# Causal attention with two full-height logit products, and the causal mask added beforehand to the subtracted row

## The chip, the cores and the metric

The kernel runs on one core of a Trainium2 chip. The metric is the device time of one execution in microseconds. A core has TensorE (PE, the products; PEld are its weight loads), VectorE (DVE), ScalarE (ACT), GpSimd (POOL) and SyncE (SP), which here issues the DMAs. Each engine works through its own queue in order and waits on semaphores for the others.

## The reference

One layer of a streaming encoder: 1024 tokens, 1024 channels, float32. A normalised input is projected once, and the columns are shared among four mixers of 256 channels each: A (mLSTM), B (causal pooling), C (RWKV) and D (forgetting attention); each has a gate, and the four go through one output projection. A cross-attention into 256 memory tokens follows. The change concerns D:

```python
def forgetting_attention(q, k, v, f_pre, qk_g):
    q = rms_norm(q, qk_g[0]) * (dh ** -0.5)
    k = rms_norm(k, qk_g[1])
    log_f_cum = jnp.cumsum(jax.nn.log_sigmoid(f_pre), axis=-1)
    for blk in range(s_len // 128):
        q0, q1 = blk * 128, (blk + 1) * 128
        logits = einsum("bhtd,bhsd->bhts", q[:, :, q0:q1], k[:, :, :q1])
        logits = logits + log_f_cum[:, :, q0:q1, None] - log_f_cum[:, :, None, :q1]
        causal = (q0 + arange(128))[:, None] >= arange(q1)[None, :]
        p = softmax(where(causal, logits, -inf))
        outs.append(einsum("bhts,bhsd->bhtd", p, v[:, :, :q1]))
```

with 4 heads of 64 channels. The term with the query's own F is the same for all keys of a row and falls out of the softmax, so the kernel subtracts only the row F of the keys.

## The kernel before, in words

**Stages.** The memory side and the first normalisation come first, then the projections of C and its recurrence. From about 480 to 565 us follow A, B and the operands of D; from 565 to 735 us attention D, into which the output projection is woven; then the cross-attention. Products in float32 precision are made of three passes with numbers split into a high and a low part: `mm3` (lines L137, L138, L139) takes high x high, high x low, low x high.

**Operands of D.** `foxop(n)` makes them, per head h. A query tile `qst[h]` of 128 rows holds the 64 channels of a head twice, as high part in one half and low part in the other; `kh[h]` holds the high part of the keys in both halves. So one product of full height (128 rows) gives q_high x k_high + q_low x k_high. The low part of the keys, `kl`, is kept once: two heads share a tile, each in one half (L1136 subtracts 64 rows). `Fb[h]` is the row F of a head, broadcast to all partitions by DMA (L1170); two heads lie side by side in one tile.

**A logit step.** `flog(g)` handles one query tile i (128 queries) and one head h, g = 4i + h. For each chunk of up to 512 of the (i+1) x 128 keys it writes one bank: L1226, the product of full height; L1227, 64 rows high, q_high x k_low; and, in the last chunk, L1229, a product of the identity with a mask that adds -1e30 above the diagonal of the last 128 columns. DVE then subtracts `Fb` and keeps the maximum (L1230), negates it (L1233), and ACT takes the exponential (L1234). `ftr(g)` transposes the weights (L1244) into a `pt` tile, `fav(g)` multiplies two heads by the values (L1257), `fin(i)` divides by the sums (L1264 to L1267) and `tgate(i)` gates the other mixers' outputs (L1206 to L1211).

**Order.** PE's instructions in D stand in an order written by hand: `flog` of the next step, two fillers, `ftr`, on even steps `fav`, then fillers again. Fillers are triples of L137 to L139: first the gate projection of D (`zgemm`, evacuated by L754 to L759), then the output projection of the tile before. DVE, ACT, POOL and SP take their instructions in the order of a scheduler with priorities. `wout(q)` loads the output weights (L1281) into `wr` and `zu` buffers and splits them (L1283 on ACT, L1284 on DVE or POOL). L126 on POOL or L124 on DVE make the low parts of the earlier weights.

**Ahead of D** on POOL stand, for each of the last chunks of A, a reciprocal root (L143, L144), for which DVE's L1067 waits, and the product with the norm's weights (L1068). DVE's evacuations of the pooling (L1119) and of `zgemm` (L754) stand behind L1067 in its queue.

Of the kernel before, what the change touches and what calls it, by code (L numbers as in the profile page):

```python
# [9 lines left out]
F32R = mybir.dt.float32r  # L10
AF = mybir.ActivationFunctionType
ALU = mybir.AluOpType
# [6 lines left out]
D = 1024  # L19
# [17 lines left out]
def tile_trunk(ctx: ExitStack, tc: tile.TileContext, a, out, dbg=None):  # L37
# [48 lines left out]
    def f32(ap):  # L86
        return ap.bitcast(F32)
# [9 lines left out]

    # ---------------------------------------------------------------- helpers
    wcount = {"wr": 0, "wh": 0, "wl": 0}
# [83 lines left out]

    # ---------------------------------------------------------------- first loads
    pr0 = tc.cur_priority
# [17 lines left out]

    # ---------------------------------------------------------------- memory side and pre norm
    mss = m0.one("mss", [128, 2])
# [73 lines left out]

    # ---------------------------------------------------------------- constants  # L280
    incl = m0.one("incl", [128, 128])
# [37 lines left out]

    # ---------------------------------------------------------------- VW = V wo per head  # L320
    def vwprep(h):
# [64 lines left out]
    def defer(n, f):  # L386
        """run f when n more of the pending projections' products are emitted."""
        after.append([n, f])

    def fill(n):  # L390
        """emit n of the pending projections' products here."""
        while n > 0 and fillers:
            try:
                w = next(fillers[0]) or 1
            except StopIteration:
                fillers.pop(0)
                continue
            n -= w
            for d in after:
                d[0] -= w  # L400
            for d in [d for d in after if d[0] <= 0]:
                after.remove(d)
                d[1]()

    def tgemm(c0, nt, evac):
        """nt tiles of 128 channels, all tokens, channels on partitions."""
        p = [[ps("mm", [128, 512]) for _ in range(2)] for _ in range(nt)]
        kk = 4 // nt
        w = wpiece(w_in, c0, nt * 128, kk)
        for _ in range(8 // kk):  # L410
            ws = [next(w) for _ in range(kk)]
            for c in range(nt):
                cs = slice(c * 128, (c + 1) * 128)
                for k, wh, wl in ws:
                    for hf in range(2):
                        mm3(p[c][hf], wh[:, cs], wl[:, cs], *hslice(k, hf * 512, 512), k == 0, k == 7)
                        yield
        for c in range(nt):
            with tc.high_priority():
                evac(c, p[c])  # L420
# [9 lines left out]
    def ngemm_q(wd, c0, n, act, evac):  # L430
        """all tokens x n columns, a bank to a token tile."""
        w = []
        for i0, ni in ((0, 2), (2, 2), (4, 4)):
            p = [ps("mm", [128, 512]) for _ in range(ni)]
            for k, wh, wl in (wpiece(wd, c0, n, 2) if i0 == 0 else w):
                if i0 == 0:
                    w.append((k, wh, wl))
                for i in range(ni):
                    mm3(p[i][:, 0:n], *act(i0 + i, k), wh, wl, k == 0, k == 7)
                    yield 0.5  # L440
            for i in range(ni):
                with tc.high_priority():
                    evac(i0 + i, p[i][:, 0:n])

    def ngemm_h(wd, c0, act, evac, nt=4):
        """all tokens x 256 columns, nt token tiles at a time."""
        w = []
        for t0 in range(0, NT, nt):
            p = [ps("mm", [128, 2, 256]) for _ in range(nt // 2)]
            for k, wh, wl in (w or wpiece(wd, c0, 256, 2)):  # L450
                if t0 == 0 and nt < NT:
                    w = w + [(k, wh, wl)]
                for i in range(nt):
                    mm3(p[i // 2][:, i % 2, :], *act(t0 + i, k), wh, wl, k == 0 and i % 2 == 0, k == 7, True)
                    yield
            for i in range(nt):
                evac(t0 + i, p[i // 2][:, i % 2, :])
# [3 lines left out]

    # ---------------------------------------------------------------- C projections
    shifted, act = [None] * 7, {}
# [28 lines left out]
    def cnorm(hf, j):  # L492
        """the keys of a head divided by their length."""
        ck, hs = shifted[2 + j], slice(hf * 512, (hf + 1) * 512)
# [232 lines left out]

    # ---------------------------------------------------------------- other projections
    def vgemm(c0, n, gc0, dst):
# [97 lines left out]

    # ---------------------------------------------------------------- gate rows, (token tile, head) on partitions
    fd = dp.tile([32, 128], F32, name="fd")
# [174 lines left out]

    # ---------------------------------------------------------------- mixers A and B, operands of D
    da = Pool("da", {"q": 4, "k": 4, "kl": 2})
    am = Pool("am", {"v": 2, "e": 3, "nu": 2, "hh": 2, "hsq": 1, "ks": 2})
# [9 lines left out]

    ab = Pool("ab", {"u": 8})
    # ---------------------------------------------------------------- A
    aqT, akT = [[t[:, q, :] for q in range(2)] for t in aqk]  # L1020
# [62 lines left out]

    # ---------------------------------------------------------------- B
    ub = []
# [35 lines left out]

    qst, kh, kl = [None] * 4, [None] * 4, [None] * 2

    def foxop(n):
        """queries (n < 4) as a stack of both parts, keys as two copies of the first part and the second part."""
        h = n % 4
        r1, r2 = PH[h % 2], PH[1 - h % 2]
        raw = ab("u", [128, 1024])
        for r in PH:
            SY.dma_start(raw[r], rT[(n // 4) * 256 + h * 64:(n // 4) * 256 + (h + 1) * 64, :])  # L1130
        hi = da("k" if n >= 4 else "q", [128, 1024], F32R)
        SC.copy(hi, raw)
        if n >= 4:
            if h % 2 == 0:
                kl[h // 2] = da("kl", [128, 1024], F32R)
            V.tensor_tensor(kl[h // 2][r1], raw[r1], f32(hi[r1]), op=ALU.subtract)  # L1136
            kh[h] = hi
        else:
            V.tensor_tensor(hi[r2], raw[r2], f32(hi[r2]), op=ALU.subtract)
            qst[h] = hi  # L1140
# [4 lines left out]
    with tc.manual_schedule(engines={PE}):  # L1145
# [17 lines left out]
        while fillers:  # L1163
            fill(1)
    Fb = []
    for h in range(4):
        if h % 2 == 0:
            fb2 = eh("t", [128, 2, 1024])
        t = fb2[:, h % 2, :]
        SY.dma_start(t.rearrange("p (a b) -> p a b", a=8),  # L1170
                     bass.AP(tensor=fd.tensor, offset=fd.offset + h * 128, ap=[[0, 128], [512, 8], [1, 128]]))
        Fb.append(t)
    ab.close()
    am.close()
    db = Pool("db", {"v": 2, "lg": 2, "pt": 4, "rE": 1})
    identr, maskN = db.one("identr", [128, 128], F32R), db.one("maskN", [128, 128], F32R)
    V.tensor_copy(identr, ident)
    V.tensor_scalar(maskN, maskD, NEG, None, op0=ALU.mult)
    dv = [db("v", [128, 4, 256]) for _ in range(2)]
    for q in range(2):  # L1180
        SY.dma_start(dv[q], dvd.rearrange("(q i p) c -> q p i c", q=2, p=128)[q])

    # ---------------------------------------------------------------- D and the output projection
    p0 = Pool("p0", {"ld": 1, "zt": 1, "act": 2})
# [29 lines left out]
    def flog(g):  # L1214
        i, h = divmod(g, 4)
        j, x = divmod(h, 2)
        ts, n, r1 = slice(i * 128, (i + 1) * 128), (i + 1) * 128, PH[x]
        if h == 0:
# [4 lines left out]
        for k, c0 in enumerate(range(0, n, 512)):  # L1223
            c1 = min(c0 + 512, n)
            p = ps("lg", [128, 512])
            T.matmul(p[:, 0:c1 - c0], qst[h][:, ts], kh[h][:, c0:c1], start=True, stop=False)  # L1226
            T.matmul(p[:, 0:c1 - c0], qst[h][r1, ts], kl[j][r1, c0:c1], start=False, stop=c1 < n)  # L1227
            if c1 == n:
                T.matmul(p[:, i * 128 - c0:n - c0], identr, maskN, start=False, stop=True)  # L1229
            V.tensor_tensor_reduce(lg[:, c0:c1], p[:, 0:c1 - c0], Fb[h][:, c0:c1], 1.0, prev, ALU.subtract, ALU.max, mx[:, k:k + 1])  # L1230
            prev = mx[:, k:k + 1]
        ng = base("tf", [128, 1])
        V.tensor_scalar(ng, prev, -1.0, None, op0=ALU.mult)  # L1233
# [81 lines left out]
    with tc.manual_schedule(engines={PE}):  # L1315
# [72 lines left out]

        # ------------------------------------------------------------ memory attention
        gcols = [cst[:, 184 + k:185 + k] for k in range(8)]  # L1390
# [6 lines left out]
        def qgemm(g):  # L1397
            """the queries of a head, channels on partitions."""
            w = []
# [123 lines left out]
def _pack(a):  # L1523
    """An identity and the vectors that go along partitions, 128 channels to a column; the pool weights as diagonal blocks."""
    import numpy as np
# [32 lines left out]
```

## Time and profile before

Three runs of the kernel took 984.74, 983.16 and 980.48 us, the median being 983.16. The profile was taken in one more execution.

| | |
|---|---|
| span of the profiled execution | 981.5 us |
| median of the runs | 983.16 us |
| PE busy | 929.1 us, 95% of the span, 6089 products |
| DVE busy | 578.9 us, 59% |
| ACT busy | 419.6 us, 43% |
| POOL busy | 252.9 us, 26% |
| A, B and operands of D, 480 to 565 us | PE busy 79.61 of 85.00 |
| D and output projection, 600 to 690 us | PE busy 90.00 of 90.00 |
| mask products L1229 in D | 32, 328 ns each by the profile |
| half-height products L1227 in D | 48, 324 to 496 ns each by width |

In a row of the timeline stand the start, the duration, engine, line and operation, what is written and read, the shape, and in brackets the idle time before it with what ended it. Products overlap in PE's pipeline and their ends are modelled, so the time that a product takes is read from one start to the next, not from its duration. Rows by line give the busy time of the group and the mean of one in ns; rows of waits give the sum, the number and the longest.

### The profile page before, as it was taken

Reading aid. Unit: us, or ns where it says so; the run is one execution under the profiler, and the core shown is the slowest. Engines: PE = TensorE matmul, PEld = TensorE weight load, DVE = VectorE, ACT = ScalarE, POOL = GpSimd, SP = SyncE. Lnnn points to the kernel's source line nnn. Section 1 sums busy time; section 2 is a strip of 40 time slices with the busy share of each in tenths; the row PEclk is TensorE's granted clock in tenths of the full one; section 3 lists DMA queues with packets and bytes.
Section 4 is the critical chain, followed back from the end, with each engine's and each line's share of the span. In section 5 each row is a group of like instructions: output and inputs, shape, how many; then the busy total and the mean of one; then the engine's idle time right before and its main releaser. Section 6 shows DMA issues by size and latency. Waiting matters only on the chain. (4 is left out here: it accounts for less than half of the span.)

```text
span 981.5 us, 16277 instructions
## 1 busy us (share of the span) xinstructions
PE 929.1 (95%) x6089; PEld 772.7 (79%) x6089; DVE 578.9 (59%) x1291; ACT 419.6 (43%) x974; POOL 252.9 (26%) x254
## 2 busy tenths in 40 slices
PE   6989999797998999999898999999999999999997
PEld 6987887586778877777776776777778788889997
DVE  6773136788696135794498747655556546654226
ACT  6666255231154333653435245433345434443321
POOL 4554224452220224454233412000000000121211
PEclk9999999798999999999899999999999999999999
DMA  7867321102324402322566675432217311125104
GB/s 241 265 212 262 107 54 34 32 22 72 75 66 123 115 28 87 111 80 87 150 158 159 198 258 188 131 100 76 75 46 245 105 35 55 44 67 198 38 12 172
DMA packets 94447, 112.53 MB, mean 115 GB/s; under 512 B 20705, under 2 KB 72993, under 8 KB 94369
## 3 DMA queue, kind: packets, MB, share of 16 engines
q1 hardware_dynamic: 94368, 111.50, 36.5%
q8 instruction: 48, 0.79, 0.3%
q14 instruction: 31, 0.25, 0.1%
HBM read 82.61 MB, written 28.87 MB: 114 GB/s over the span
## 5 line engine op out<-in xcount | busy, mean ns | idle before, releaser
L126 POOL TENSOR_TENSOR wl<-wr,wh 128x512 fp32r<-128x512 f32 (+2 forms) x98 | 139.9, 1430 | 401.8 <-ACT wh L122 385.0
L137 PE MATMUL mm<-h,wh 128*128 128x512 f32 x528 | 219.6, 416 | 0.2 <-DVE zu L754 0.2
L139 PE MATMUL mm<-h,wl 128*128 128x512 f32 x528 | 208.8, 395 | 0.0
L138 PE MATMUL mm<-l,wh 128*128 128x512 f32 x528 | 208.6, 395 | 0.0
L137 PEld LDWEIGHTS mm<-h,wh 128*128 128x128 f32 x528 | 99.9, 189 | 24.3 <-issue 1.9
L139 PEld LDWEIGHTS mm<-h,wl 128*128 128x128 f32 x528 | 99.9, 189 | 22.9
L122 ACT CAST wh<-wr 128x512 fp32r<-128x512 f32 (+2 forms) x122 | 74.7, 619 | 97.5 <-PE mm L138 32.9
L138 PEld LDWEIGHTS mm<-l,wh 128*128 128x128 f32 x528 | 100.2, 190 | 17.4 <-issue 0.5
L137 PE MATMUL mm<-wh,act 128*128 128x256 f32 x256 | 71.7, 280 | 0.0
L138 PE MATMUL mm<-wl,act 128*128 128x256 f32 x256 | 70.9, 277 | 0.0
L139 PE MATMUL mm<-wh,act 128*128 128x256 f32 x256 | 70.8, 277 | 0.0
L137 PE MATMUL mm<-h,act 128*128 128x512 f32 x128 | 54.7, 427 | 0.0
L139 PE MATMUL mm<-h,act 128*128 128x512 f32 x128 | 50.5, 394 | 0.0
L138 PE MATMUL mm<-l,act 128*128 128x512 f32 x128 | 50.4, 394 | 0.0
L137 PEld LDWEIGHTS mm<-wh,act 128*128 128x128 f32 x256 | 48.2, 188 | 0.1
L138 PEld LDWEIGHTS mm<-wl,act 128*128 128x128 f32 x256 | 48.1, 188 | 0.0
L139 PEld LDWEIGHTS mm<-wh,act 128*128 128x128 f32 x256 | 48.0, 188 | 0.0
L137 PE MATMUL mm<-wh,h 128*128 128x260 f32 (+1 forms) x128 | 39.2, 306 | 1.5 <-DVE zu L819 1.5
L137 PE MATMUL mm<-mT,wh 128*128 128x256 f32 x128 | 37.6, 293 | 1.4 <-ACT wh L122 1.4
L139 PE MATMUL mm<-mT,wl 128*128 128x256 f32 x128 | 37.1, 290 | 1.4 <-DVE wl L124 1.4
L139 PE MATMUL mm<-wh,l 128*128 128x260 f32 (+1 forms) x128 | 38.1, 298 | 0.0
L138 PE MATMUL mm<-wl,h 128*128 128x260 f32 (+1 forms) x128 | 38.0, 297 | 0.0
(407 smaller groups left out, 2020.2 us busy)
## 6 DMA issues: line engine op xcount, KB each, us to landing
wr<-in_w_in_dram SPq DMA_DIRECT2D x50, 256.0 KB, 2.9
wr<-in_xattn_wkv_dram SPq DMA_DIRECT2D x32, 256.0 KB, 3.8
x<-in_x_dram SPq DMA_DIRECT2D x16, 512.0 KB, 4.7
x<-x1d SPq DMA_DIRECT2D x15, 512.0 KB, 5.6
wr<-in_xattn_wo_dram SPq DMA_DIRECT2D x16, 256.0 KB, 3.0
vwd<-row SPq DMA_DIRECT2D x8, 512.0 KB, 3.9
rT<-zu SPq DMA_DIRECT2D x16, 256.0 KB, 2.4
zT<-zu SPq DMA_DIRECT2D x16, 256.0 KB, 3.2
```

What stands on the lines that cost most here:

```text
L122: SC.copy(hi, raw)
L126: G.tensor_tensor(lo, raw, f32(hi), op=ALU.subtract)
L137: T.matmul(o, lh, rh, start=st, stop=False, skip_group_check=skip)
L138: T.matmul(o, lh, rl, start=False, stop=False, skip_group_check=skip)
L139: T.matmul(o, ll, rh, start=False, stop=sp, skip_group_check=skip)
```

## The change

The low part of the keys becomes a tile of 128 rows per head, the same 64 channels in both halves, so that the second product has full height too: it gives q_high x k_low + q_low x k_low. The identity, the mask tile and the product L1229 go. The mask takes another way: `maskD` (1 above the diagonal) is multiplied by 1e30, and POOL adds it in place to the 128 columns of `Fb` that lie on the diagonal of each query tile, for two heads at once: 16 additions ahead of D. When the second head of a pair has read its block, a DMA of 128 KB writes the plain row there again, since the next query tiles read the block without a mask. To make room there are four `kl` tiles instead of two, six load buffers `u` instead of eight, and three `pt` tiles instead of four.

```diff
-    da = Pool("da", {"q": 4, "k": 4, "kl": 2})
+    da = Pool("da", {"q": 4, "k": 4, "kl": 4})
...
-    ab = Pool("ab", {"u": 8})
+    ab = Pool("ab", {"u": 6})
...
         if n >= 4:
-            if h % 2 == 0:
-                kl[h // 2] = da("kl", [128, 1024], F32R)
-            V.tensor_tensor(kl[h // 2][r1], raw[r1], f32(hi[r1]), op=ALU.subtract)
+            kl[h] = da("kl", [128, 1024], F32R)
+            V.tensor_tensor(kl[h], raw, f32(hi), op=ALU.subtract)
...
-    db = Pool("db", {"v": 2, "lg": 2, "pt": 4, "rE": 1})
-    identr, maskN = db.one("identr", [128, 128], F32R), db.one("maskN", [128, 128], F32R)
-    V.tensor_copy(identr, ident)
-    V.tensor_scalar(maskN, maskD, NEG, None, op0=ALU.mult)
+    db = Pool("db", {"v": 2, "lg": 2, "pt": 3, "rE": 1})
+    V.tensor_scalar(maskD, maskD, -NEG, None, op0=ALU.mult)
+    for i in range(NT):
+        for j in range(2):
+            t = Fp[j][:, :, i * 128:(i + 1) * 128]
+            G.tensor_tensor(t, t, maskD[:, None, :].to_broadcast([128, 2, 128]), op=ALU.add)
...
             T.matmul(p[:, 0:c1 - c0], qst[h][:, ts], kh[h][:, c0:c1], start=True, stop=False)
-            T.matmul(p[:, 0:c1 - c0], qst[h][r1, ts], kl[j][r1, c0:c1], start=False, stop=c1 < n)
-            if c1 == n:
-                T.matmul(p[:, i * 128 - c0:n - c0], identr, maskN, start=False, stop=True)
+            T.matmul(p[:, 0:c1 - c0], qst[h][:, ts], kl[h][:, c0:c1], start=False, stop=True)
             V.tensor_tensor_reduce(lg[:, c0:c1], p[:, 0:c1 - c0], Fb[h][:, c0:c1], 1.0, prev, ALU.subtract, ALU.max, mx[:, k:k + 1])
             prev = mx[:, k:k + 1]
+        if h % 2 and i < NT - 1:
+            SY.dma_start(Fp[j][:, :, ts], bass.AP(tensor=fd.tensor, offset=fd.offset + (4 * i + 2 * j) * 128, ap=[[0, 128], [128, 2], [1, 128]]))
```

The instructions move at three places. On PE, the logit step of query tile 3, head 0 (512 keys in one chunk; `lg` is the PSUM bank, `k` and `kl` are the high and low part of the keys, `q` the queries; the rows L137 to L139 are fillers), stood before as

```order
L138 MATMUL mm_6409<-l_6051,act_6335 128x512
L139 MATMUL mm_6409<-h_6050,act_6336 128x512
L1226 MATMUL lg_6472<-k_5483,q_5033 128x512
L1227 MATMUL lg_6472<-kl_5485,q_5033 128x512
L1229 MATMUL lg_6472<-maskN,identr 128x128
L137 MATMUL mm_6483<-h_6177,act_6335 128x512
L138 MATMUL mm_6483<-l_6178,act_6335 128x512
```

and stands now, between the same fillers, as

```order
L138 MATMUL mm_6418<-l_6064,act_6345 128x512
L139 MATMUL mm_6418<-h_6063,act_6346 128x512
L1229 MATMUL lg_6481<-k_5483,q_5033 128x512
L1230 MATMUL lg_6481<-kl_5485,q_5033 128x512
L137 MATMUL mm_6491<-h_6189,act_6345 128x512
L138 MATMUL mm_6491<-l_6190,act_6345 128x512
```

The mask product is gone; nothing else on PE changes its place in D. (The lines of the changed kernel are a few numbers higher.)

On POOL, at the last two chunks of A (`tm`, `hh`) and the last weights of the projections (`wl`), stood before

```order
L1068 TENSOR_TENSOR hh_5639<-hh_5639,na_g 128x256
L126 TENSOR_TENSOR wl_5942<-wr_5939,wh_5941 128x512
L143 TENSOR_SCALAR tm_5733<-tm_5731 128x4
L144 TENSOR_TENSOR tm_5733<-tm_5733,mhalf 128x4
L1068 TENSOR_TENSOR hh_5727<-hh_5727,na_g 128x256
L126 TENSOR_TENSOR wl_5970<-wr_5967,wh_5969 128x512
L1284 TENSOR_TENSOR l_6051<-wr_6052,h_6050 128x512
```

and now the additions (`t`, the two tiles of the row F) stand between:

```order
L1068 TENSOR_TENSOR hh_5640<-hh_5640,na_g 128x256
L1181 TENSOR_TENSOR t_5838<-t_5838,maskD 128x2x128 x8
L126 TENSOR_TENSOR wl_5956<-wr_5953,wh_5955 128x512
L143 TENSOR_SCALAR tm_5734<-tm_5732 128x4
L144 TENSOR_TENSOR tm_5734<-tm_5734,mhalf 128x4
L1068 TENSOR_TENSOR hh_5728<-hh_5728,na_g 128x256
L1181 TENSOR_TENSOR t_5841<-t_5841,maskD 128x2x128 x8
L126 TENSOR_TENSOR wl_5983<-wr_5980,wh_5982 128x512
L1287 TENSOR_TENSOR l_6064<-wr_6065,h_6063 128x512
```

So eight additions stand ahead of the last reciprocal root of A (L143, L144), and eight ahead of the last L126.

On SP, at the start of D, behind the loads of the values (`v`), stood before

```order
L1181 DMA v_5852<-dvd 128x4x256
L1197 DMA ld_6026<-yu 128x512
L1198 DMA zt_6027<-zT 128x2x128
L1199 DMA zt_6027<-ybT 128x2x128
L1281 DMA wr_6052<-in_w_out_dram 128x512
L1281 DMA wr_6060<-in_w_out_dram 128x512
L1281 DMA zu_6038<-in_w_out_dram 128x512
L1281 DMA zu_6046<-in_w_out_dram 128x512
```

and now the first two restores stand among these loads:

```order
L1184 DMA v_5867<-dvd 128x4x256
L1234 DMA t_5838<-fd 128x2x128
L1200 DMA ld_6039<-yu 128x512
L1201 DMA zt_6040<-zT 128x2x128
L1202 DMA zt_6040<-ybT 128x2x128
L1284 DMA wr_6065<-in_w_out_dram 128x512
L1284 DMA wr_6073<-in_w_out_dram 128x512
L1284 DMA zu_6051<-in_w_out_dram 128x512
L1234 DMA t_5841<-fd 128x2x128
L1284 DMA zu_6059<-in_w_out_dram 128x512
```

The first restore waits for the reduction of tile 0, head 1, the second for that of head 3; what stands behind each is issued after it.

More of the change, by code (lines that the diff above doesn't have):

```diff
@@ L1120, in bpool @@
         SY.dma_start(ybT[j * 128:(j + 1) * 128, :], zb)
-    qst, kh, kl = [None] * 4, [None] * 4, [None] * 2
+    qst, kh, kl = [None] * 4, [None] * 4, [None] * 4
     def foxop(n):
         h = n % 4
-        r1, r2 = PH[h % 2], PH[1 - h % 2]
+        r2 = PH[1 - h % 2]
         raw = ab("u", [128, 1024])
@@ L1164, in tile_trunk @@
             fill(1)
-    Fb = []
+    Fb, Fp = [], []
     for h in range(4):
@@ L1168, in tile_trunk @@
             fb2 = eh("t", [128, 2, 1024])
+            Fp.append(fb2)
         t = fb2[:, h % 2, :]
@@ L1215, in flog @@
         i, h = divmod(g, 4)
-        j, x = divmod(h, 2)
-        ts, n, r1 = slice(i * 128, (i + 1) * 128), (i + 1) * 128, PH[x]
+        j = h // 2
+        ts, n = slice(i * 128, (i + 1) * 128), (i + 1) * 128
         if h == 0:
```

## The prediction

> **What bounds the kernel now.** I read the table of windows first, then who waits for whom on TensorE, then its timeline. The attention D with the output projection (565 to 735 us) is where the change works.
>
> ```profile
> 565.00:600.00 35.00, 33.16 (x153) 25.05 (x154) 21.56 (x53) 17.25 (x40) 7.60 (x6) 1.00 0.68 227
> 600.00:640.00 40.00, 40.00 (x224) 29.34 (x223) 24.16 (x64) 17.46 (x42) 4.16 (x6) 1.00 0.51 162
> 690.00:735.00 45.00, 45.00 (x270) 32.83 (x269) 24.57 (x66) 19.08 (x37) 2.16 (x4) 1.00 0.18 57
> ```
>
> The columns are the stretch, its length, then busy time of PE, PEld, DVE, ACT and POOL, the granted clock, the DMA share and GB/s. From 600 us on PE is busy in every microsecond; DVE with 24.57 of 45 and ACT with 19.08 have room. Over the whole stage PE waits for others only here:
>
> ```profile
> PE tr L1267 <- DVE zt L1208: 1.7, 1, 1.7
> PE mm L137 <- DVE zu L754: 0.2, 1, 0.2
> ```
>
> So D is bound by PE alone, and what leaves PE's sequence there leaves the span, unless the start of D comes later. The wait of the weight loads shows what is dear in a logit step (columns: us in total, times, longest):
>
> ```profile
> PEld lg L1227 <- issue: 10.9, 38, 0.4
> PEld lg L1229 <- issue: 3.4, 16, 0.3
> ```
>
> The half-height second product (64 rows) and the mask product wait for nothing but PE itself. Ends of products are modelled, so I go by starts. First two neighbours of full height, 512 wide, then a logit step of query tile 3 up to the second filler behind it:
>
> ```profile
> 565.66 0.39 PE L139 MATMUL mm<-h,wl 128*128 128x512 f32 x1
> 565.89 0.39 PE L137 MATMUL mm<-h,wh 128*128 128x512 f32 x1
> 635.69 0.40 PE L1226 MATMUL lg<-k,q 128*128 128x512 f32 x1
> 636.02 0.50 PE L1227 MATMUL lg<-kl,q 64*128 64x512 f32 x1
> 636.44 0.33 PE L1229 MATMUL lg<-maskN,identr 128*128 128x128 f32 x1
> 636.61 0.45 PE L137 MATMUL mm<-h,act 128*128 128x512 f32 x1
> 636.89 0.40 PE L138 MATMUL mm<-l,act 128*128 128x512 f32 x1
> ```
>
> A full-height product takes 0.23 us from start to start (565.66 to 565.89). Ahead of the half-height product the step takes 0.33, behind it 0.42: each change of height costs 0.1 to 0.2 us. The Trainium skill agrees (TensorEngine Tiling (Array Packing), "Key Properties": a change of the tiling mode drains the engine). Its page TensorE: Matmul & The Clock Gate, Part 3, would make half height cheap instead, since products in different row groups can overlap; here they don't, at 0.42 against 0.23, so by that rule nothing but the mask row would be saved, which is rival C.
>
> **The sum, part by part.**
>
> *Logit steps.* Tile 3: 635.69 to 636.89 is 1.20; afterwards two products and one filler at 0.23 are 0.69, so 0.51 is saved; I take 0.50 for tiles 1 to 3. The short and the long end:
>
> ```profile
> 573.53 0.22 PE L1226 MATMUL lg<-k,q 128*128 128x128 f32 x1
> ...
> 574.38 0.40 PE L138 MATMUL mm<-l,wh 128*128 128x512 f32 x1
> 731.21 0.40 PE L1226 MATMUL lg<-k,q 128*128 128x512 f32 x1
> ...
> 733.27 0.39 PE L138 MATMUL mm<-l,act 128*128 128x512 f32 x1
> 575.70 0.11 PE tr L1244
> ```
>
> Tile 7 takes 2.06 with two chunks; four products and a filler at 0.23 are 1.15: 0.91 saved. Tile 0 takes 0.85 with products 128 wide. For the pitch of these the bounds are a quarter of 0.23 (0.06) and the 0.11 of a 128-wide transpose in the chain of waits: 0.40 to 0.50 saved, I take 0.44. Tiles 4 to 6 lie between, with a narrower last chunk than tile 7: 0.84, 0.88, 0.88. Four heads each: 4 x (0.44 + 3 x 0.50 + 0.84 + 2 x 0.88 + 0.91) = **21.8 us**, with an uncertainty of about 1.5 from the pitches.
>
> *Keys and buffers.* The subtraction that makes the low part now covers 128 rows instead of 64 at the same 1024 columns:
>
> ```profile
> L1136 DVE TENSOR_TENSOR kl<-u,k 64x1024 fp32r<-64x1024 f32 x4 | 5.1, 1267 | 0.1
> L1306 DVE SCALAR_TENSOR_TENSOR y<-y,tt,x 128x1024 f32<-128x1024 f32 x8 | 10.3, 1284 | 2.8 <-POOL tt L1305 2.7
> 568.01 0.22 DVE L1177 CAST identr<-cst 128x128 fp32r<-128x128 f32 x1
> ```
>
> 128 rows of 1024 take 1.28 where 64 take 1.27, so nothing is added; were it by rows, four times 1.3 would come to DVE, ahead of 540 us, where it is not the bound. Six load buffers instead of eight: the new waits are on conversions that ended before those loads went out, so nothing (at worst one conversion of 1.3 on a load, under other work). Three buffers of transposed weights instead of four: in PE's order at most three are in use when the next is written, and the PE waits above show none for them: nothing, or up to the 1.7 of its longest wait. Two small DVE operations go (such as L1177, 0.22); that helps DVE at 568 us and I count nothing for it.
>
> *Mask added on POOL.* Sixteen additions of 128x256 elements, in two lots of eight. The first lot stands behind the normalisation product of mLSTM chunk 6 and ahead of the reciprocal root of chunk 7; POOL and DVE there:
>
> ```profile
> 553.29 0.73 POOL L1068 TENSOR_TENSOR hh<-hh,na_g 128x256 f32<-128x256 f32 x1 [0.59 <-issue]
> 555.79 1.39 POOL L126 TENSOR_TENSOR wl<-wr,wh 128x512 fp32r<-128x512 f32 x1 [1.78 <-ACT wh L122]
> 557.54 1.01 POOL L144 TENSOR_TENSOR tm<-tm,mhalf 128x4 f32<-128x4 f32 x1
> 559.14 0.74 POOL L1068 TENSOR_TENSOR hh<-hh,na_g 128x256 f32<-128x256 f32 x1 [0.59 <-PE mm L139]
> 564.87 1.29 POOL L126 TENSOR_TENSOR wl<-wr,wh 128x512 fp32r<-128x512 f32 x1 [4.98 <-ACT wh L122]
> 558.58 0.42 DVE L1067 TENSOR_TENSOR hh<-hh,tm 128x256 f32<-128x256 f32 x1 [1.63 <-POOL tm L144]
> 564.28 0.75 DVE L754 TENSOR_SCALAR zu<-mm,pc 128x512 f32<-128x512 f32 x1
> 565.09 0.50 PE L137 MATMUL mm<-h,wh 128*128 128x512 f32 x1 [0.15 <-DVE zu L754]
> L1068 POOL TENSOR_TENSOR hh<-hh,na_g 128x256 f32<-128x256 f32 x8 | 8.1, 1018 | 4.1 <-PE mm L139 1.2 <-DMA wr<-in_w_in_dram 1.1 <-DVE hh L1067 0.6
> L722 POOL TENSOR_TENSOR yc<-yc,tc x8: 612/614/1042, 351.3 to 462.4; 128x256 f32<-128x256 f32 x8
> ```
>
> An addition of this size takes 0.61 (L722, the least) to 1.02 (L1068, the mean); at 0.73, as the undisturbed L1068, eight take 5.8. They start at 554.0 and end at 559.9 (558.9 to 562.2). From the start of L126 to the end of L144 POOL took 555.79 to 558.55, or 2.76, so L144 ends at 562.6 instead of 558.55: 4.1 later. DVE's L1067 waits for it, and behind L1067 in DVE's queue stand the evacuations up to L754 (564.28), for which the first product of D waits at 565.09. PE therefore stands still some 4 us (3 to 6). The second lot starts when chunk 7 is done, about 564, and holds the last L126 and with it the buffer into which the next output weights are loaded: about 5 us later, with the first need of them 13 us behind.
>
> *Clock.* A stall of that length has a second price:
>
> ```profile
> 220.00:225.00 5.00, 1.84 (x16) 1.63 (x14) 4.95 (x5) 0.62 (x1) 3.67 (x3) 0.97 0.40 109
> 225.00:230.00 5.00, 4.86 (x27) 4.31 (x27) 1.79 (x9) 0.26 (x1) 0.00 (x0) 0.50 0.15 47
> ```
>
> After 3.2 us without PE work the granted clock was 0.50 in the next 5 us, which costs up to 2.5. I take 1 (0 to 2.5), since the stall here may be just under or over that. The Trainium skill has the same rule (TensorE: Matmul & The Clock Gate, Part 1, idle gaps over some 3.4 us throttle the array); the trace agrees with it as far as this place goes.
>
> *What the late start is worth.* At 592 the profile has a chain into the first transposes of the output projection:
>
> ```profile
> 577.23 0.70 ACT zu L756
> ...
> 581.69 1.70 POOL l L1284
> 583.40 4.61 DMA zu<-in_w_out_dram
> ```
>
> It begins behind a PE product (577), so it is late by what PE is late there: 4.0 + 1.0 less the four logit steps of tile 0 (4 x 0.44 = 1.8), or 3.2; PE itself then has two more logit steps saved and its own wait of 1.7 in hand, so the chain decides. I take **+3.0** at that point (from -0.5, all absorbed, to +7). Behind it stand 26 logit steps, 21.8 - 1.8 - 2 x 0.50 = 19.0.
>
> *Restores.* Fourteen DMAs of 128 KB write the plain row back, and each waits in SP's queue for an odd head's reduction. Behind the first stand the loads of `ld` and `zt` for tile 0 and four of the output weights, which ACT's and POOL's splits wait for.
>
> ```profile
> 570.08 0.29 DVE L1230 CUSTOM_DVE_ANT_0 lg<-lg,t 128x128 f32<-128x128 f32 x1
> 584.05 0.41 DVE L1230 CUSTOM_DVE_ANT_0 lg<-lg,t 128x256 f32<-128x256 f32 x1
> v<-avd SPq DMA_DIRECT2D x8, 128.0 KB, 3.6
> ```
>
> The block freed at 570.08 is read again at 584.05; issue and landing of a load of this size take about 4, so 10 us are left. I count them at nothing. The loads behind the first restore go out with the late reduction, some 4 us later than now, which is inside the +3.0.
>
> *Sum.* -19.0 + 3.0 = -16.0. The profiled execution has a span of 981.5, 1.7 below the median of 983.16; nothing here is a share of the whole, so I take the difference off the median: **967 us**.
>
> **Rivals.**
> A. The start of D gives back more: eight additions at 1.02 (8.2 us), DVE's operations stretched beside them, the clock at half for 5 us: +7 to +10 at the first output projection, 971 to 974. For it: POOL's rows next to busy DVE, 1.02 against 0.73. Against: PE has slack at 592.
> B. The late start is wholly absorbed: 19.0 + 2.8 off, 961.4. For it: 1.7 of wait at 592 and idle time on every other engine. Against: the chain that begins at 577 is PE's own.
> C. The edit doesn't do what it says: the time lies in the second product itself and not in its height. Then only the mask rows go: 32 x 0.17 (636.44 to 636.61) = 5.4, less 3: 981. Against: 0.42 for 512 columns, where 0.23 is usual.
> D, the slower side. The restores become the bound: if a restore reaches the row later than about 14 us after its reduction, each of 14 next steps waits on DVE, then PE. With e over that, 14 x e is added: from e = 1.5 on (21 us against 16 saved) the kernel is slower, 988. For it: pieces of 512 bytes, and a queue with loads in it. Against: 3.6 to land, with a DMA share of 0.18 to 0.51 from 600 us on.
>
> **How the numbers follow.** My forecast (963 to 971) has a chance of 0.68, A 0.13, B 0.10, C 0.05, D 0.04. Leaving out C and D and the far end of A, the range is 960 to 974. A measurement here can tell about 0.5%, or 5 us, from no change. Faster by more than that: my forecast, A and B, 0.91; within 0.5%: C, 0.05; slower: D, 0.04.
>
> **What would show it.** The logit step of tile 3 should take 0.69 from its first product to the second filler behind it, that of tile 7 1.15, with no waits of the weight loads on the second product. The first product of D should start at 569 to 570 and wait for L754's successor, with a lower granted clock in the next 5 us if the stall is over 3 us. From 600 us on PE should stay busy all the time, and no DVE reduction should wait for a DMA. If reductions wait for the restores, or if the second product still takes 0.4, I am wrong.

## The result, and the profile after

The changed kernel took 966.26 us (median of four runs, 964.24 to 968.87) beside 982.19 for the kernel before (four runs, 980.48 to 984.74): a ratio of 0.9837 with a 95% interval of 0.981 to 0.9864. A second set of runs gave 0.9844 (0.9819 to 0.9868). The forecast was 967 us. The profiled execution has a span of 967.0 us.

First the logit steps, in PE's timeline of the changed kernel: tile 3, then tile 0, then tile 7, each from its first product to the second filler.

```profile
635.72 0.39 PE L1229 MATMUL lg<-k,q 128*128 128x512 f32 x1
635.95 0.40 PE L1230 MATMUL lg<-kl,q 128*128 128x512 f32 x1
636.18 0.39 PE L137 MATMUL mm<-h,act 128*128 128x512 f32 x1
636.41 0.39 PE L138 MATMUL mm<-l,act 128*128 128x512 f32 x1
...
575.83 0.22 PE L1229 MATMUL lg<-k,q 128*128 128x128 f32 x1
575.89 0.27 PE L1230 MATMUL lg<-kl,q 128*128 128x128 f32 x1
576.00 0.45 PE L137 MATMUL mm<-h,wh 128*128 128x512 f32 x1
576.28 0.39 PE L138 MATMUL mm<-l,wh 128*128 128x512 f32 x1
...
717.82 0.39 PE L1229 MATMUL lg<-k,q 128*128 128x512 f32 x1
...
718.97 0.40 PE L138 MATMUL mm<-l,act 128*128 128x512 f32 x1
```

Tile 3 takes 0.69 (1.20 before), tile 7 1.15 (2.06), tile 0 0.45 (0.85). The two 128-wide products started 0.06 and 0.11 apart, the two ends that the prediction had set for them.

Then POOL, DVE and PE at the start of D:

```profile
551.96 0.73 POOL L1068 TENSOR_TENSOR hh<-hh,na_g 128x256 f32<-128x256 f32 x1 [0.59 <-issue]
552.65 5.78 POOL L1181 TENSOR_TENSOR t<-t,maskD 128x256 f32<-128x256 f32 x8
...
560.04 1.02 POOL L144 TENSOR_TENSOR tm<-tm,mhalf 128x4 f32<-128x4 f32 x1
...
562.34 6.98 POOL L1181 TENSOR_TENSOR t<-t,maskD 128x256 f32<-128x256 f32 x8
561.10 0.42 DVE L1067 TENSOR_TENSOR hh<-hh,tm 128x256 f32<-128x256 f32 x1 [5.13 <-POOL tm L144]
567.39 0.74 DVE L754 TENSOR_SCALAR zu<-mm,pc 128x512 f32<-128x512 f32 x1
568.18 0.51 PE L137 MATMUL mm<-h,wh 128*128 128x512 f32 x1 [2.71 <-DVE zu L754]
```

This execution was 1.3 us ahead of the one before when chunk 6 of A was done (551.96 against 553.29 at L1068), so I measure from there. Eight additions took 5.78 us, DVE waited 5.13 for the root (1.63 before), and the first product of D came 16.2 us after L1068 instead of 11.8: 4.4 us late. Part of the wait (1.57) shows one product earlier, at the pooling; 2.71 show here.

Then PE's waits from 560 to 740 us:

```profile
PE mm L137 <- DVE zu L754: 2.7, 1, 2.7
PE tr L1270 <- DVE zt L1211: 2.2, 1, 2.2
PE ml L1118 <- DVE u L1119: 1.6, 1, 1.6
PE mm L137 <- ACT jk L1305: 0.7, 1, 0.7
PE mm L137 <- ACT zu L756: 0.3, 1, 0.3
PE tr L1247 <- ACT lg L1237: 0.2, 1, 0.2
```

The first and the third are the late start. The second stood in the list before with 1.7; the last three are new. The windows around the first output projection, and one behind it (the clock is the third column from the end):

```profile
590.00:595.00 5.00, 2.77 (x15) 1.92 (x15) 3.60 (x9) 3.47 (x7) 1.27 (x1) 0.89 0.84 277
595.00:600.00 5.00, 5.00 (x19) 3.86 (x18) 3.86 (x9) 2.29 (x5) 1.02 (x1) 0.77 0.59 179
640.00:690.00 50.00, 50.00 (x337) 41.35 (x336) 31.19 (x93) 22.39 (x48) 2.19 (x4) 1.00 0.31 96
```

From 640 us on PE is busy all the time, as before, with 337 products in 50 us instead of 286. The clock fell at the first output projection, not at 568. The weight loads no longer wait at the logit products: the 14.3 us of L1227 and L1229 are not in the list of the changed kernel.

The chain of waits into the first transposes of the output projection:

```profile
572.15 0.29 DVE lg L1231
...
573.23 0.62 SPq L1234
573.95 0.70 SPq L1200
574.70 0.75 SPq L1201
575.50 0.53 SPq L1202
576.08 6.95 DMA wr<-in_w_out_dram
...
593.49 0.41 PE tr L1270 x2
```

The first restore (L1234) does stand on the path: it waited for the late reduction, and the weights behind it came later. The transposes start at 593.49, or 41.5 us after L1068; before it was 38.9.

For all kernels below I use one measure that leaves out the scatter of the stages before and after: the **stretch** from L1068 of chunk 6 on POOL to the first product of the last logit step. Before it is 553.29 to 731.21, or 177.9 us; in the changed kernel 551.96 to 717.82, or 165.9, and 165.4 in its second profile. Two profiles of one kernel differ by up to 1.7.

### The profile page after: what moved, and what is told of

It reads as the page before. It is cut to its first block, busy times and chain, and to the rows that moved or that the text cites. A ratio compares the mean times of both kernels' runs of the same rounds, so it can differ in the third digit from the quotient of the medians.

```text
span 967.0 us, 16286 instructions
## 1 busy us (share of the span) xinstructions
PE 911.7 (94%) x6057; PEld 769.8 (80%) x6057; DVE 577.0 (60%) x1290; ACT 419.6 (43%) x974; POOL 264.3 (27%) x270
## 5 line engine op out<-in xcount | busy, mean ns | idle before, releaser
L126 POOL TENSOR_TENSOR wl<-wr,wh 128x512 fp32r<-128x512 f32 (+2 forms) x98 | 140.4, 1435 | 395.4 <-ACT wh L122 380.3
L137 PE MATMUL mm<-h,wh 128*128 128x512 f32 x528 | 221.5, 419 | 3.0 <-DVE zu L754 2.7
L138 PE MATMUL mm<-l,wh 128*128 128x512 f32 x528 | 210.9, 399 | 0.0
L139 PE MATMUL mm<-h,wl 128*128 128x512 f32 x528 | 210.8, 399 | 0.0
L137 PEld LDWEIGHTS mm<-h,wh 128*128 128x128 f32 x528 | 101.0, 191 | 27.7 <-DVE zu L754 3.1
L139 PEld LDWEIGHTS mm<-h,wl 128*128 128x128 f32 x528 | 101.2, 192 | 23.4
L137 PE MATMUL mm<-wh,act 128*128 128x256 f32 x256 | 71.8, 281 | 0.0
L139 PE MATMUL mm<-wh,act 128*128 128x256 f32 x256 | 70.8, 277 | 0.0
L137 PE MATMUL mm<-h,act 128*128 128x512 f32 x128 | 53.6, 419 | 0.7 <-ACT jk L1305 0.7
L139 PE MATMUL mm<-h,act 128*128 128x512 f32 x128 | 50.4, 394 | 0.0
L137 PEld LDWEIGHTS mm<-wh,act 128*128 128x128 f32 x256 | 48.2, 188 | 0.1
L139 PEld LDWEIGHTS mm<-wh,act 128*128 128x128 f32 x256 | 48.0, 188 | 0.0
L137 PE MATMUL mm<-wh,h 128*128 128x260 f32 (+1 forms) x128 | 39.4, 308 | 1.5 <-DVE zu L819 1.5
L137 PE MATMUL mm<-mT,wh 128*128 128x256 f32 x128 | 37.5, 293 | 1.4 <-ACT wh L122 1.4
L139 PE MATMUL mm<-mT,wl 128*128 128x256 f32 x128 | 37.1, 290 | 1.6 <-DVE wl L124 1.6
L139 PE MATMUL mm<-wh,l 128*128 128x260 f32 (+1 forms) x128 | 38.1, 298 | 0.0
```

The lines of the kernel that those rows point to most:

```text
L126: G.tensor_tensor(lo, raw, f32(hi), op=ALU.subtract)
L137: T.matmul(o, lh, rh, start=st, stop=False, skip_group_check=skip)
L138: T.matmul(o, lh, rl, start=False, stop=False, skip_group_check=skip)
L139: T.matmul(o, ll, rh, start=False, stop=sp, skip_group_check=skip)
```

## The experiments

**1. The height alone.** The low keys at full height as in the change, the mask still a product, no additions, no restores.

```diff
-    V.tensor_scalar(maskD, maskD, -NEG, None, op0=ALU.mult)
-    for i in range(NT):
-        for j in range(2):
-            t = Fp[j][:, :, i * 128:(i + 1) * 128]
-            G.tensor_tensor(t, t, maskD[:, None, :].to_broadcast([128, 2, 128]), op=ALU.add)
+    identr, maskN = onesr, maskD
+    V.tensor_copy(identr, ident)
+    V.tensor_scalar(maskN, f32(maskD), NEG, None, op0=ALU.mult)
...
-            T.matmul(p[:, 0:c1 - c0], qst[h][:, ts], kl[h][:, c0:c1], start=False, stop=True)
+            T.matmul(p[:, 0:c1 - c0], qst[h][:, ts], kl[h][:, c0:c1], start=False, stop=c1 < n)
+            if c1 == n:
+                T.matmul(p[:, i * 128 - c0:n - c0], identr, maskN, start=False, stop=True)
...
-        if h % 2 and i < NT - 1:
-            SY.dma_start(Fp[j][:, :, ts], bass.AP(tensor=fd.tensor, offset=fd.offset + (4 * i + 2 * j) * 128, ap=[[0, 128], [128, 2], [1, 128]]))
```

> Second logit product at full height as in the change, but the mask stays a product of identity and mask tile, and nothing is added to or restored in the row F. If the change of height is what is dear: a step of tile 3 goes from 1.20 us to 0.80-0.86 (two products at 0.23, the mask at 0.11 to 0.17, a filler at 0.23), all steps together save 21.8 - 32 x 0.14 = 17.3 us, D starts as early as before (565 us, no long PE wait there), and the time is 965 us (963 to 967). If the mask row was the dear part and not the height: 980 to 982.

Measured: 0.9826 of before (0.9801 to 0.9851), 966.07 us. The step of tile 3 in its timeline:

```profile
630.29 0.39 PE L1227 MATMUL lg<-k,q 128*128 128x512 f32 x1
630.52 0.39 PE L1228 MATMUL lg<-kl,q 128*128 128x512 f32 x1
630.75 0.22 PE L1230 MATMUL lg<-maskD,onesr 128*128 128x128 f32 x1
630.81 0.45 PE L137 MATMUL mm<-h,act 128*128 128x512 f32 x1
631.10 0.41 PE L138 MATMUL mm<-l,act 128*128 128x512 f32 x1
```

0.81 us, 0.12 more than in the changed kernel and 0.39 less than before. The stretch is 163.2 us. The height alone gives the whole gain. (Identity and mask take over the tiles of `onesr` and `maskD`; the numbers of buffers are those of the change.)

**2. The mask alone.** The second product keeps its half height (the low keys are made in two tiles again, which is left out below); additions, restores and the buffers `u` and `pt` as in the change.

```diff
-            T.matmul(p[:, 0:c1 - c0], qst[h][:, ts], kl[h][:, c0:c1], start=False, stop=True)
+            r1 = PH[h % 2]
+            T.matmul(p[:, 0:c1 - c0], qst[h][r1, ts], kl[j][r1, c0:c1], start=False, stop=True)
```

> The second logit product keeps its half height, the mask is added beforehand and restored as in the change. If the height is dear: a step of tile 3 takes about 1.03 us (1.20 less the 0.17 of the mask row), 32 x 0.17 = 5.4 us saved, less 3 to 4 at the late start of D: 979 to 981 us. If the mask row was the dear part: 966 to 970.

Measured: 1.0001 (0.9986 to 1.0017), 983.45 us; stretch 177.6, so 0.4 less than before. I had expected 979 to 981. The step of tile 3:

```profile
634.31 0.40 PE L1231 MATMUL lg<-k,q 128*128 128x512 f32 x1
634.64 0.50 PE L1233 MATMUL lg<-kl,q 64*128 64x512 f32 x1
635.07 0.50 PE L137 MATMUL mm<-h,act 128*128 128x512 f32 x1
635.41 0.40 PE L138 MATMUL mm<-l,act 128*128 128x512 f32 x1
```

It takes 1.10, only 0.10 less than before. The mask row had taken 0.17, but behind it the filler cost 0.28; now the filler itself follows the half-height product and costs 0.34. So 32 steps give some 3.2 us, and the late start of D takes most of them back: the first logit product comes 19.8 us after L1068, as in the change, and 15.4 before it. The buffers of the change bring nothing by themselves.

**3. The additions spread.** The changed kernel, with the two additions for tile 0 ahead of D and those for tile i+1 issued at tile i, and POOL's order written by hand in D (the scheduler would otherwise move them all ahead again).

```diff
-    for i in range(NT):
+    def fmask(i):
         for j in range(2):
             t = Fp[j][:, :, i * 128:(i + 1) * 128]
             G.tensor_tensor(t, t, maskD[:, None, :].to_broadcast([128, 2, 128]), op=ALU.add)
...
-    with tc.manual_schedule(engines={PE}):
+    with tc.manual_schedule(engines={PE, mybir.EngineType.Pool}):
         fill(6)
+        fmask(0)
         flog(0)
         for g in range(4 * NT):
             i, h = divmod(g, 4)
+            if h == 0 and i + 1 < NT:
+                fmask(i + 1)
```

> The changed kernel with the 16 additions spread: two ahead of D (one of them ahead of the last reciprocal root of A), those of tile i+1 during tile i. If the additions in POOL's queue make D start late: the first product of D comes 0.7 to 1 us later than in the kernel before instead of 4, PE's wait for L754 there falls below 1 us, and the time is 962.5 us (960.5 to 964.5). If the start of D is held by something else (the weights, SP's queue): 966, as the change.

Measured: 0.9805 (0.9771 to 0.984), 964.41 us; stretch 161.6. The first logit product comes 15.4 us after L1068, exactly as before the change, where the changed kernel has 19.8. But PE then waits longer at the first output projection (from the list of the spread kernel):

```profile
PE tr L1271 <- DVE zt L1212: 3.5, 1, 3.5
PE mm L137 <- DVE zu L754: 1.2, 2, 1.0
```

4.4 us were won at the start of D, 2.9 were left at the first transposes (38.6 after L1068 against 41.5).

**4. Without the restores.**

```diff
-        if h % 2 and i < NT - 1:
-            SY.dma_start(Fp[j][:, :, ts], bass.AP(tensor=fd.tensor, offset=fd.offset + (4 * i + 2 * j) * 128, ap=[[0, 128], [128, 2], [1, 128]]))
```

> The changed kernel without the restores: later tiles read the row F with the mask still in it, so most keys are masked away. If the first restores hold back the loads of the output weights behind them in SP's queue: those loads go out 1 to 3 us earlier and the first transposes of the output projection with them, 964 us (963 to 965). If the restores are hidden: 966, within 0.1%. If restores were on the path of every tile: below 960.

Measured: 0.9841 (0.9809 to 0.9872), 968.37 us; stretch 166.2. Neither of the times that were named came out. In this execution the granted clock also fell behind the wait at the start of D (0.83 from 565 to 575), which it had not done in the change, and the first logit product came 21.4 us after L1068 instead of 19.8. The first transposes came at 43.4; without the 1.5 us of that fall it would be some 41.8, beside 41.5 in the change. So the loads set free did not bring the output projection earlier: PE still waited 2.5 us there. Behind it PE waits no more, and from the third head of tile 1 to the first product of tile 3 this kernel takes 23.6 us, the change 25.1 and, in its second profile, 24.9. What the restores cost as a whole is therefore not settled: some 1 us may be hidden here behind the fall of the clock.

**5. The same three side by side, and the restores on another queue.** The change, the height alone and the spread additions were timed again in five rounds beside a fourth kernel, in which ACT instead of SP issues the restores, behind the exponential.

> The changed kernel itself, on the same chip as the three below: 0.984 of before (0.982 to 0.986).

> Full height with the mask still a product, once more beside the change. If the mask's part of the change is worth what its rows took (0.12 us in each of 32 steps, 3.8 us) less what its additions cost at the start of D (4.4 us): equal to the change or up to 0.1% faster, 0.983 (0.981 to 0.985). If the mask's part is a gain: 0.3% slower than the change or more.

> The additions spread over D, once more beside the change and the height alone. If the mask's part gains its 3.8 us once its additions don't delay D: 0.3 to 0.4% faster than the change, 0.980 (0.978 to 0.982). If the earlier look was scatter: 0.984.

> The additions spread over D, and the 14 restores issued from ACT's queue behind the exponential instead of SP's. If restores in SP's queue hold back the loads of the output weights: PE's wait at the first transposes of the output projection falls from 3.5 us to 2 or less, 0.978 to 0.979. If the restores are hidden: 0.980, as with SP's queue. If issuing them (0.4 us each) delays ACT's conversions: 0.981 to 0.983.

| kernel | ratio to before | stretch, us |
|---|---|---|
| before | 1 | 177.9 |
| the change | 0.9844 (0.9819 to 0.9868) | 165.4 |
| the height alone | 0.981 (0.9782 to 0.9838) | 161.5 |
| additions spread | 0.981 (0.9784 to 0.9837) | 162.4 |
| spread, restores by ACT | 0.9824 (0.98 to 0.9848) | 161.7 |

The stretch in each row is that of one profile, and that of the kernel before is the one from above. The intervals overlap. By the stretch, the height alone (161.5 and 163.2) and the spread additions (161.6 and 162.4) stand 2.2 to 4.4 us ahead of the change (165.4 and 165.9), and level with each other. Part of this lead is the clock: behind the first transposes it fell in both profiles of the change (1.6 us), and in one of the two of either other kernel. The height alone was expected at most 0.1% faster than the change and came out 0.3% faster.

Why the spread additions are no better than the height alone can be read from two places. From the first product of tile 3 to the last step they are 2.1 us faster (94.6 against 96.7), the worth of the mask products there. But they reach tile 3 67.0 and 67.8 us after L1068, the height alone 66.5 and 64.8. Whether the additions or the restores cost them this is not shown. With the restores on ACT's queue the first transposes come 35.6 us after L1068, 3 earlier than in the spread kernel, but the stretch ends no earlier. Its longest PE waits show where that went:

```profile
PE mm L137 <- ACT jk L1306: 2.3, 1, 2.3
PE mm L137 <- DVE zu L754: 1.9, 2, 1.8
PE tr L1271 <- DVE zt L1212: 0.6, 1, 0.6
```

**6. Two restores on ACT, twelve on SP.** The edit is shown against the kernel with all restores on ACT.

```diff
-            SC.dma_start(Fp[j][:, :, ts], bass.AP(tensor=fd.tensor, offset=fd.offset + (4 * i + 2 * j) * 128, ap=[[0, 128], [128, 2], [1, 128]]))
+            (SY if i else SC).dma_start(Fp[j][:, :, ts], bass.AP(tensor=fd.tensor, offset=fd.offset + (4 * i + 2 * j) * 128, ap=[[0, 128], [128, 2], [1, 128]]))
```

> The additions spread over D, the two restores of tile 0 issued from ACT's queue and the other twelve from SP's. From the additions' place (the norm product of chunk 6 of A) to the last logit step the spread kernel took 161.6 and 162.4 us, the one with all restores on ACT 161.7, though its first output projection came 3 us earlier there. If SP's first restores hold back the output weights and ACT's later restores took that gain away again: about 159 us for this stretch, 0.978 of before. If the gain at the first output projection is lost whoever issues the later restores: 162 us, 0.981.

Measured: 0.9842 (0.9801 to 0.9884), 967.96 us; stretch 161.4, not 159. The first transposes come 37.0 after L1068, then PE waits 1.8 for the last evacuation of the gate projection (L754). So in both kernels in which ACT issues restores the gain at the first output projection turns into waits soon behind it. The ratio is worse than the stretch because this execution lost time elsewhere (252.5 us from the last logit step's first product to the end, 250.3 before).

**7. The change with the mask product kept as well.** Here `onesr` is the identity times -1, and `maskD` holds 1e30 above the diagonal.

```diff
+    V.tensor_scalar(onesr, ident, -1.0, None, op0=ALU.mult)
...
+            if c1 == n:
+                T.matmul(p[:, i * 128 - c0:n - c0], onesr, maskD, start=False, stop=True)
```

> The changed kernel with the mask product kept as well (the mask is then subtracted twice, which changes nothing in the softmax). If a full-height mask product is worth 0.12 us a step, as the steps of the height-only kernel show: 32 x 0.12 = 3.8 us slower than the change, the stretch from the norm product of chunk 6 to the last logit step takes 169.5 us instead of 165.4 to 165.9, 0.988 of before. If D hides it: 165.7 us, 0.984.

Measured: 0.9881 (0.9839 to 0.9922), 970.03 us; stretch 167.1 instead of 169.5. Behind the third head of tile 1 the rest of the stretch takes 122.5 us against 119.7 in the change: 2.7 for 25 steps, or 0.11 each, as expected. The first transposes come 41.6 us after L1068, as in the change (41.5), in spite of six more products and of a clock that fell at the start of D: PE waited 0.2 there instead of 2.2. So ahead of that place the mask product is hidden in a wait. The third head of tile 1 then comes 1.5 us earlier than in the change, since the clock did not fall behind the transposes here.

**The part where PE never waits.** From the first product of tile 3 to that of the last step PE waits for no other engine in any of the four kernels below, and the granted clock is 1.00. So this part shows the two halves of the change without the rest:

| second product | mask | us |
|---|---|---|
| half height (before) | product | 109.6 |
| half height (experiment 2) | added | 107.5 |
| full height (experiment 1) | product | 96.7 |
| full height (the change) | added | 94.6 |

The height is worth 12.9 us with either mask, the mask 2.1 with either height.

## Why the prediction was right, point by point

**The logit steps** were right to 0.01 us: 0.69 and 1.15 as forecast, and 0.45 for tile 0, whose saving of 0.40 is the lower end (0.44 taken). What saves is the height: 0.39 of the 0.51 of tile 3, by experiment 1, namely 0.10 ahead of the second product, 0.19 behind it and 0.11 behind the mask product. The mask row adds 0.12 once the height is even, and 0.10 while it is not (experiment 2). Rival C, that the height costs nothing and only the mask rows go, falls in both of its parts: the height is nearly all, and the mask rows were worth less than the 5.4 us set down for them.

That the price lies in the change of height, and not in the half height itself, is what the prediction said without showing it; the trace of the kernel before has a place that does. In the preparation of C, products of 64 rows and 512 columns stand beside each other, three in each half of the rows:

```profile
160.02 0.50 PE L138 MATMUL sm<-sp,lora 64*128 64x512 f32 x1 [0.23 <-DVE sp L161]
160.03 0.50 PE L137 MATMUL sm<-sp,lora 64*128 64x512 f32 x1
160.36 0.39 PE L139 MATMUL sm<-sp,lora 64*128 64x512 f32 x1
160.36 0.39 PE L138 MATMUL sm<-sp,lora 64*128 64x512 f32 x1
160.60 0.39 PE L139 MATMUL sm<-sp,lora 64*128 64x512 f32 x1
160.91 0.50 PE L137 MATMUL mm<-h,wh 128*128 128x512 f32 x1
```

Products of the two halves start 0.00 to 0.01 us apart, and two of one half 0.24 (160.36 to 160.60), as at full height. So "here they don't" overlap holds for the logit step, where the half-height product stands alone between full ones, and not for this kernel as a whole.

**The additions** took 5.78 us as forecast (5.8), and the first product of D came 4.4 late (4.1 worked out, "some 4" forecast). That they cause it is shown by experiment 3, where the start of D is back where it was.

**The clock.** The price was there, in another place. The prediction expected it behind the stall at the start of D. It fell behind the second wait, at 593.5, where eight products went by at some 0.43 from start to start instead of 0.23:

```profile
594.05 0.63 PE L138 MATMUL mm<-l,wh 128*128 128x512 f32 x1
594.48 0.63 PE L139 MATMUL mm<-h,wl 128*128 128x512 f32 x1
...
597.38 0.39 PE L137 MATMUL mm<-h,wh 128*128 128x512 f32 x1
...
598.08 0.28 PE L1229 MATMUL lg<-k,q 128*128 128x256 f32 x1
```

From the transposes (593.49) to the tenth filler product behind them (597.38) it took 3.9 us, before 2.3: 1.6 for the 1.0 in the sum. That the price came due at all is in part luck, since the stall for which it was set down did not bring it. (The earlier stall, read as 3.2 us, is 3.3 by PE's waits.)

**The first transposes** came 2.7 us late (41.5 against 38.9 after L1068; +3.0 forecast). The forecast held the 1.0 for the clock, which had not fallen by then; without it 2.2 were worked out. The path was not quite the one forecast: in the kernel before it began with a product of PE at 577, here it leads through the late reduction and the first restore in SP's queue. With the clock's 1.6 behind them, the place after which PE runs densely is 4.2 late: the third head of tile 1 starts 46.1 after L1068, before it was 41.9.

**The rest** was over-estimated. 19.0 us were to be saved behind the first transposes. From the third head of tile 1 to the last step the trace shows 119.7 instead of 136.1, or 16.3, and with the last step itself (0.9) 17.2. Tiles 3 to 7 saved what was worked out (2.06 for tile 3 against 2.0, 3.56 for tile 6 against 3.52); tile 2 and the end of tile 1 gave 1.35 instead of 3.0, with a new wait of 0.7 for the first output tile's squares (L1305). In the kernel without restores the same part gave 2.9. So "from 600 us on PE should stay busy all the time" held only from 640 on: the term was mis-sized, not the mechanism.

**The sum.** In D the trace shows 12.1 and 0.9, some 13 us, where 16 were forecast; the medians differ by 15.9 and, in the second set, by 14.7. Of the 3 us, 1.2 lie ahead of the third head of tile 1 (4.2 late, +3.0 in the sum), half of it the clock, and 1.8 behind it, in tiles 1 and 2. That the time itself hit 967 within 1 us is in part luck: this execution was 1.3 us ahead at L1068, a place that lies at 550.9 in one profile of the height-only kernel and at 553.8 in the other, and the interval of the first set reaches from 13.4 to 18.7 us.

**The restores** were counted at nothing. Up to the first transposes experiment 4 bears this out, though the first restore stands on the path at 573; for tiles 1 and 2 it leaves some 1 us open. No reduction waited for a DMA; rival D did not occur.

What the prediction did not ask is whether the mask's part of the change pays at all. It doesn't: its product is worth at most 3.8 us, some of it hidden, and its additions cost 4.4 at the start of D, of which 2.9 are left at the first transposes. With the product kept and only the height changed, the kernel is as fast as the best version found, and simpler.

## What to carry to other kernels

Ahead of a half-height product between full ones, and behind it, the start-to-start time grew by 0.1 to 0.2 us each, together more than a product 512 wide takes (0.23); filling the other half with something harmless was faster than sparing the rows. Whether half-height products of two heads side by side would do as well was not tried. A saving in PE's sequence is counted only from the place where PE stops waiting; ahead of it, a shorter step is worth nothing until the chain that PE waits for is shorter. Work that is moved to an idle engine is to be looked up in that engine's queue: what stands right behind it, and who waits for that.

## What the runs showed of the hardware

The granted clock falls in some executions and not in others, after the same wait. These are the windows of 565 to 600 us of two executions of the height-only kernel, which both waited 2.1 us at the first transposes, first the one, then the other:

```profile
565.00:600.00 35.00, 32.58 (x162) 25.45 (x161) 21.96 (x54) 17.25 (x41) 7.11 (x5) 0.95 0.69 219
```

```profile
565.00:600.00 35.00, 32.52 (x163) 25.35 (x162) 22.86 (x53) 18.08 (x42) 8.44 (x6) 1.00 0.73 242
```

Their stretches are 163.2 and 161.5, so the fall costs about 1.7 us; 1.6 of it lie between the first transposes and the third head of tile 1 (4.6 us against 3.0). In the changed kernel a wait of 2.7 at 568 left the clock alone and one of 2.2 at 593 brought it down; in experiment 7 it fell behind the wait at D's start (0.73 from 565 to 570). In the two profiles of the spread additions a wait of 3.5 at the first transposes left it at 1.00, and one of 3.0 brought it to 0.50 for 5 us. The Trainium skill (TensorE: Matmul & The Clock Gate, Part 1) gives a gap of some 3.4 us as the point from which it happens. Here waits of 2.0 to 3.0 were enough at times, and ones of 2.1, 2.7 and 3.5 were not. What decides was not tried.
